# Head queries and keys taken straight from PSUM, a new order of the first phase, and a mix loaded by feature tiles

## The chip, the cores and the metric

The kernel runs on one core of a Trainium2 chip. The metric is the device time of one execution in microseconds; where several executions were timed, the median is given. The engines are named as in the profile: PE is TensorE (matmuls), DVE VectorE, ACT ScalarE, POOL GpSimd, SP SyncE, which issues nearly all transfers.

## The reference, cut to what matters

One layer of a streaming encoder runs over 1056 tokens: 1024 of a prompt and 32 of a running stream, 1024 features each. The layer has an adaLN modulation, one input projection shared by three groups of heads, an output projection with a LayerNorm, then a SwiGLU feed-forward part with another.

```python
h = x * (1 + sc1) + sh1
mq, mk, mv, mo, mi, mf, fq, fk, fv, ff, gu, gv = jnp.split(h @ w_in, split_at, axis=-1)
logf = jax.nn.log_sigmoid(ff + b_fox_f)          # gates of the attention heads
hm, (C1, n1, m1) = _mlstm(...)                   # 4 heads, chunks, decaying matrix memory
# 8 attention heads ("fox") of width 64, causal, with a forget term on the scores:
logits = q @ k.T * 64 ** -0.5 + Ft[:, None] - Ft[None, :]     # Ft = cumsum(logf)
hf = softmax(where(causal, logits, -inf)) @ v
hg = _spatial_gate(gu, layer_norm(gv), ws, bs)   # gMLP
mix = concat([hm, hf, hg], -1) @ w_o
x = layer_norm(ALPHA * x + (1 + g1) * mix)
```

The keys and values of the attention heads, the gates and the mLSTM's last state are outputs too (`o_kT` holds the keys).

## The kernel before

**Precision.** Each large product is done as three matmuls in the type fp32r. An operand is split into a high part (a cast by ACT) and a low part (the remainder, by DVE), and `gemm` (L111) multiplies hi·hi, hi·lo and lo·hi per tile of 128 features (L117 to L119). A weight tile of 512 KB is loaded and split in `weights` (L94; L105 on ACT, L106 on DVE).

**Memory.** Outputs of matmuls go to PSUM banks out of four pools: `pg` with three banks for projections, `pt` with two, `pss` with two for attention scores, `po` with one. A bank comes free when the last engine has read it. Tiles in the on-chip memory come from pools too; a pool that is closed gives its space to the one opened next, so that the later pool's first write waits for the earlier pool's last use. A pool's `bufs` is the length of a tile's ring.

**Order.** The program order is not the order in which the engines work: a scheduler in the compiler moves the instructions and then fixes, for each engine, one order in which it goes through its instructions; waits are on semaphores. `high_priority` puts a part ahead. The order of units in the first phase is the string `ORDER` (L42), read left to right by `run` (L1245): `q` a head's query/key projection, `f` the attention of one head over the first 512 tokens, `k0` and `k1p` the mLSTM's keys, `s` the states of the mLSTM (`mlstm_states`, L499), `v` and `o` the mLSTM's value and output-gate projections, `m` one of its chunks, `a` one unit of the adaLN modulation (`ada`, L171). `f` and `m` have high priority.

**Stages**, in the profile's times. Up to 105 us: modulation, the modulated tokens `h1`, the mLSTM's first projection, the value units. From 105 to 163: the first heads' projections and `gates` (L386). `gates` takes logarithms of the gates, cumulates them on PE (L426 and L427), then runs a long chain of small DVE operations (L433 to L487), stores the sums for the heads (`dfs`), d0 (`dd0`) and M (`dM`), and transposes the result on PE (L492) into `col`, whose exponential is L495. From 163 to 379: the eight heads' attention (`fox`, L672, `fox_chunk`, L699), woven with the mLSTM and from 290 on with the gMLP units (`tm_unit`, L272, with the evictions `evac_gv`, L343, and `evac_gmlp`, L639). From 379: the output projection of the first 512 tokens (`wo`, L942) with its LayerNorm; heads 4 to 7 of the other tokens until 462 us; then the feed-forward part.

**A head's way, before.** `fm_unit` (L236) computes 128 rows (64 of queries, 64 of keys) for pieces of 256 or 272 tokens. For heads 0 and 1 (`QD` = 2) all four pieces are done at once, for the others the first two, and the second two after the gMLP. `evac_qk` (L359) empties each bank: ACT writes the high part (L366), DVE the low part (L367), POOL their sum (L368), and three transfers store high, low and the keys. `fox` then loads from these stores what the scores need: `k1` (the keys' high part twice), `qp` (the queries' high and low part), `k2` and `q2` (the rest, with four rows of cumulated gates from `dfs`) and `v`, nine transfers in all. `foxbufs` (L1317) gives the rings of these tiles: k1 2, qp and q2 1, k2 1, v 3. They lie in the pool `mx0`, which is opened right after the gates' pool is closed. Each row of scores is two matmuls (L717 and L718) into a `pss` bank; DVE adds the mask and takes the maximum, ACT the exponential (L726). The probabilities are transposed on PE (L753) and multiplied by `v`; ACT and DVE add two halves (L773, L774) and the result is stored to `dmix`.

**The mix.** The three groups write the concatenated mix to DRAM (`dmix`). For the output projection, `wo_res` (L937) loads x (8 transfers of 256 KB), then `wo_mix` (L926) loads the mix: for each half of 256 tokens and each of the 8 feature tiles one transfer of 128 KB into a ring of four tiles, from which ACT writes the high part (L934) and DVE the low (L935). Feature tiles 2, 3, 4, 5, 0 and 1 are asked for first, 6 and 7 (the gMLP's) after the second pieces of heads 2 and 3.

Of the kernel before, what the change touches and what calls it, by code (L numbers as in the profile page):

```python
# [7 lines left out]
F32 = mybir.dt.float32  # L8
F32R = mybir.dt.float32r
AF = mybir.ActivationFunctionType  # L10
ALU = mybir.AluOpType
# [4 lines left out]
P = 128  # L16
D = 1024
KT = 8
# [7 lines left out]
QD = 2  # L26
# [12 lines left out]
MLB = (1, 2, 3, 4, 5)  # L39
RESE = "pp"  # L40
TAFF = ("aaaaaaaa", "aaaaaaav")
ORDER = "q0 f0 q1 a f1 a q2 f2 k0 k1p s a q3 f3 a v q4 f4 a q5 f5 o a m0 q6 f6 a m1 q7 m2 f7 a m3"  # L42
ADAPOS = 4
GENG = (0, 1, 1, 0)
FP = (0, 0)
# [20 lines left out]
def f(ap):  # L66
    return ap.bitcast(F32)


class Kernel:  # L70
# [288 lines left out]
    def evac_qk(self, h):  # L359
        nc = self.nc  # L360

        def evac(o, n, ps):
            hi = self.t(self.sm, [P, 272], F32R, "qkh", 3)
            lo = self.t(self.sm, [P, 272], F32R, "qkl", 2)
            kr = self.t(self.sm, [P, 272], F32, "qkr", 3)
            nc.scalar.activation(hi[:, :n], ps, AF.Copy, scale=self.qsc)  # L366
            nc.vector.scalar_tensor_tensor(lo[:, :n], ps, self.qsc, f(hi[:, :n]), ALU.mult, ALU.subtract)  # L367
            nc.gpsimd.tensor_tensor(kr[:, :n], f(hi[:, :n]), f(lo[:, :n]), ALU.add)  # L368
            self.store(self.dqh[h, :, o:o + n], f(hi[:, :n]))
            self.store(self.dql[h, :, o:o + n], f(lo[:, :n]))  # L370
            self.store(self.d["o_kT"][h, :, o:o + n], kr[64:, :n])
            if o + n == T:
                nc.gpsimd.tensor_copy(self.qks[:, h, :], kr[:, n - NS:n])
        return evac

    def evac_mqk(self, i, scale):
        nc = self.nc

        def evac(o, n, ps):
            r = self.t(self.sm, [P, 272], F32, "qkr", 3)  # L380
            nc.scalar.activation(r[:, :n], ps, AF.Copy, scale=scale)
            self.store(self.dmqk[:, i, o:o + n], r[:, :n])
        return evac
# [288 lines left out]
    def fox(self, h, chunks):  # L672
        self.phase = "fox"
        mx = self.mx
        q0, q1 = chunks[0][0] * P, (chunks[-1][-1] + 1) * P
        nq, nk, nb = q1 - q0, q1, q1 // P
        t = lambda shape, dt, tag, bufs: self.t(mx, shape, dt, tag, bufs)
        b = self.foxbufs
        k1 = t([P, nk], F32R, "k1", b[0])
        qp = t([P, nq], F32R, "qp", b[1])  # L680
        k2 = t([68, nk], F32R, "k2", b[2])
        q2 = t([68, nq], F32R, "q2", b[1])
        v = t([P, nb, P], F32R, "v", b[3])
        qs = slice(q0, q1)
        self.load(f(qp[0:64]), self.dqh[h, 0:64, qs])
        self.load(f(qp[64:128]), self.dql[h, 0:64, qs])
        self.load(f(k1[0:64]), self.dqh[h, 64:128, :nk])
        self.load(f(k1[64:128]), self.dqh[h, 64:128, :nk])
        self.load(f(q2[0:64]), self.dqh[h, 0:64, qs])
        self.load(f(q2[64:68]), self.dfs[h, 2:6, qs])  # L690
        self.load(f(k2[0:64]), self.dql[h, 64:128, :nk])
        self.load(f(k2[64:68]), self.dfs[h, 0:4, :nk])
        self.load(f(v), self.dv[:, :nb, h * P:(h + 1) * P])
        for tiles in chunks:
            o = tiles[0] * P - q0
            n = len(tiles) * P
            yield from self.fox_chunk(h, tiles, nk, n, k1, k2, qp[:, o:o + n], q2[:, o:o + n], v)

    def fox_chunk(self, h, tiles, W, nq, k1, k2, qp, q2, v):  # L699
        nc, mx = self.nc, self.mx  # L700
        nb = tiles[-1] + 1
        t = lambda shape, dt, tag, bufs: self.t(mx, shape, dt, tag, bufs)
        b5 = self.foxbufs[4]
        probs = []
        for i in tiles:
            n = (i + 1) * P
# [33 lines left out]
        o = self.t(self.po, [P, 512], F32, "o")  # L740
# [4 lines left out]
        for unit in units:  # L745
            ps = self.t(self.pt, [P, 512], F32, "t")
            at, e = [], 0
            for b in unit:
                first = max(0, b - tiles[0])
                w = nq - first * P  # L750
                for y in range(first, len(tiles)):
                    c = e + (y - first) * P
# [15 lines left out]
            self.phase = "fox"  # L768
        if held is not None:
            nc.tensor.matmul(o[:, :nq], v[:, 0, :], held[:, :nq], start=False, stop=True)  # L770
        tmp = t([64, nq], F32, "fo", 1)
        r = t([64, nq], F32, "fr", 1)
        nc.scalar.copy(tmp[:, :nq], o[64:128, :nq])  # L773
        nc.vector.tensor_tensor(r[:, :nq], o[0:64, :nq], tmp[:, :nq], ALU.add)  # L774
        c = tiles[0] // 4
        o = tiles[0] * P - GO[c]
        self.store(self.dmix[c][64 * (h % 2):64 * (h % 2) + 64, 2 + h // 2, o:o + nq], r[:, :nq])
# [148 lines left out]
    def wo_mix(self, c, ks):  # L926
        self.phase = f"wo{c}"
        nc = self.nc
        for a, b in MM[c]:
            for k in ks:  # L930
                r = self.t(self.p2, [P, 272], F32, "tmp", 4)[:, :b - a]
                self.load(r, self.dmix[c][:, k, a:b])
                h = self.hh[c][a][:, k, :b - a]
                nc.scalar.copy(h, r)  # L934
                nc.vector.tensor_tensor(self.hl[c][a][:, k, :b - a], r, f(h), ALU.subtract)  # L935
# [309 lines left out]
    def run(self):  # L1245
        nc, tc, d = self.nc, self.tc, self.d
        dr = self.pool("dr", space=DRAM)
        t = lambda shape, tag: self.t(dr, shape, F32, tag)
# [35 lines left out]
        w2, w3 = d["w_in"], d["w_in_f"]  # L1284
# [18 lines left out]
        def more(n):  # L1303
            for u in rest[:n]:
                self.ada(u, self.pl, "late", 2, self.pt, "t")
            del rest[:n]
# [7 lines left out]
        more(T1[3])  # L1314
        s2 = ExitStack()
        self.mx = self.pool("mx0", ctx=s2)
        self.foxbufs = (2, 1, 1, 2, 3)  # L1317

        def emit(x):
            eng = nc.gpsimd if x[-1] == "p" else nc.vector  # L1320
            x = x.rstrip("p")
            i = int(x[1:] or 0)
            if x[0] == "f":
                return self.fox(i, ((0, 1, 2, 3),))
            if x[0] == "m":
                return self.mlstm(i)
            if x[0] == "q":
                self.fm_unit(w3[2 + i], self.evac_qk(i), (0, 1) if i < QD else (0,), eng)
            elif x[0] == "k":
                self.fm_unit(w3[i], self.evac_mqk(2 + i, 0.125), eng=eng)  # L1330
            elif x[0] == "s":
                self.mlstm_states()
            elif x[0] == "a":
                more(1)
            else:
                self.tm_unit(w2["-vo".index(x)], 256, self.evac_raw((None, self.dmv, self.dmo)["-vo".index(x)]), eng=eng)
            return ()
# [12 lines left out]
        self.pz = self.pool("pz")  # L1350
        self.p2 = self.pada = self.pool("p2")
        self.hh, self.hl, self.z = {}, {}, {}
        self.wo_res(0, self.pz)
        self.operand(0, self.ph)
        self.wo_mix(0, self.KORDER[:6])
        def tail_ada():
            for u in rest:
                self.ada(u, self.wp, "raw", RAW, self.pg, "g")

        for i in range(4):  # L1360
            if i == ADAPOS:
# [102 lines left out]
        n = nj * 256  # L1464
        t = self.t(self.pz, [P, 4, n], F32R, "z0", 1)
        w = self.last_weights(((t[:, 0], t[:, 1]), (t[:, 2], t[:, 3])), (2, 3))
        act2 = dict(act)
        for half, (a, b) in enumerate(LN[1][::-1]):
# [6 lines left out]
            else:  # L1475
                h, l = (self.t(pb, [P, KT * 272], F32R, f"{x}{a}", 1) for x in ("ah", "al"))
# [111 lines left out]
```

## Time and profile before

| What | Value |
|---|---|
| Median of 3 runs | 1398.54 us (1397.95 to 1400.02) |
| Profiled execution, its own time | 1397.36 us |
| Its span in the trace | 1395.6 us |
| Mean granted clock of PE | 0.988 |
| From the first head projection to the output projection | 105.64 to 379.17 us |
| First matmul of the feed-forward part | 462.9 us |
| DMA engines, mean over the span | 167 GB/s |

Each line of the page's list of groups gives a source line, an engine, an operation with its tiles and its count, then the busy time, the mean of one in nanoseconds, and the idle time just before such instructions. A line of waits has the engine and the tile, after the arrow what released it, then the sum in microseconds, how often, and the longest. A line of a timeline begins with the start (us from the span's start) and the duration; a count at its end joins equal neighbours, and a bracket gives the idle time ahead and its releaser. A matmul's record overlaps with the next one's, so that durations of 0.28 us stand at starts 0.12 us apart: the spacing is what a matmul costs.

### The profile page before, as it was taken

Reading aid. Unit: us, or ns where it says so; the run is one execution under the profiler, and the core shown is the slowest. Engines: PE = TensorE matmul, PEld = TensorE weight load, DVE = VectorE, ACT = ScalarE, POOL = GpSimd, SP = SyncE. Lnnn points to the kernel's source line nnn. Section 1 sums busy time; section 2 is a strip of 40 time slices with the busy share of each in tenths; the row PEclk is TensorE's granted clock in tenths of the full one; section 3 lists DMA queues with packets and bytes.
Section 4 is the critical chain, followed back from the end, with each engine's and each line's share of the span. In section 5 each row is a group of like instructions: output and inputs, shape, how many; then the busy total and the mean of one; then the engine's idle time right before and its main releaser. Section 6 shows DMA issues by size and latency. Waiting matters only on the chain.

```text
span 1395.6 us, 25879 instructions
## 1 busy us (share of the span) xinstructions
PE 1346.8 (97%) x9651; PEld 1238.7 (89%) x9651; DVE 1034.0 (74%) x2198; ACT 641.6 (46%) x1257; POOL 258.7 (19%) x292
## 2 busy tenths in 40 slices
PE   7999999999979799999999999999999999999996
PEld 4899988899979778888887889899999999999996
DVE  5548646678779657777776766678997988888777
ACT  3313234445445444545544445344673544545355
POOL 0103200052146500000000000264620000000341
PEclk9999999999999899999999999999999999999998
DMA  9764577585755656444443342555597767563321
GB/s 360 255 219 134 171 234 210 176 253 168 225 174 158 186 174 178 128 131 138 137 131 85 100 119 83 198 153 139 157 237 202 204 174 199 149 174 112 101 91 65
DMA packets 134709, 233.09 MB, mean 167 GB/s; under 512 B 22436, under 2 KB 77356, under 8 KB 134584
## 3 DMA queue, kind: packets, MB, share of 16 engines
q1 hardware_dynamic: 129272, 221.34, 51.3%
q0 software_dynamic: 5168, 9.96, 4.6%
q8 instruction: 76, 1.25, 0.4%
q14 instruction: 49, 0.40, 0.1%
q10 hardware_dynamic: 144, 0.14, 0.0%
HBM read 197.50 MB, written 53.81 MB: 180 GB/s over the span
## 4 chain that ended last, share of the span: by engine, by line
PE 68%; DVE 4%; DMA 3%; issue 1%; ACT 1%; SPq 0%; POOL 0%; DVEq 0%; ACTq 0%
PE up_g L117 5%; PE up_g L118 5%; PE up_g L119 5%; PE dn_g L119 4%; PE dn_g L117 4%; PE dn_g L118 4%; PE sup_u L119 3%; PE sup_u L117 3%; PE sup_u L118 3%; PE wo_g L117 2%; PE wo_g L118 2%; PE wo_g L119 2%; PE sup_g L118 2%; PE sup_g L119 2%; PE sup_g L117 2%; PE fox_t L753 2%
## 5 line engine op out<-in xcount | busy, mean ns | idle before, releaser
L117 PE MATMUL up_g<-mlstm_ah,up_whi 128*128 128x512 f32 (+1 forms) x384 | 142.4, 371 | 4.3 <-ACT lna_tmp L996 3.4
L118 PE MATMUL up_g<-mlstm_al,up_whi 128*128 128x512 f32 (+1 forms) x384 | 142.8, 372 | 0.6 <-DVE mlstm_al L1001 0.6
L119 PE MATMUL up_g<-mlstm_ah,up_wlo 128*128 128x512 f32 (+1 forms) x384 | 142.2, 371 | 0.0
L284 PE MATMUL tm_g<-tm_whi,start_h1l 128*128 128x256 f32 (+1 forms) x384 | 110.0, 287 | 0.0
L282 PE MATMUL tm_g<-tm_whi,start_h1h 128*128 128x256 f32 (+1 forms) x384 | 109.6, 287 | 0.0
L283 PE MATMUL tm_g<-tm_wlo,start_h1h 128*128 128x256 f32 (+1 forms) x384 | 109.5, 286 | 0.0
L117 PE MATMUL fm_g<-start_h1h,fm_whi 128*128 128x256 f32 (+2 forms) x344 | 101.9, 301 | 4.7 <-DVE fm_qkl L367 2.0
L118 PE MATMUL fm_g<-start_h1l,fm_whi 128*128 128x256 f32 (+2 forms) x344 | 101.6, 295 | 0.2 <-DVE start_h1l L223 0.2
L119 PE MATMUL fm_g<-start_h1h,fm_wlo 128*128 128x256 f32 (+2 forms) x344 | 100.8, 294 | 0.0
L1120 ACT CAST sup_whi<-sup_raw 128x1024 fp32r<-128x1024 f32 x54 | 56.0, 1048 | 90.3 <-PE dn_u L118 46.7
L117 PEld LDWEIGHTS up_g<-mlstm_ah,up_whi 128*128 128x128 f32 x384 | 74.2, 193 | 16.6 <-ACT mlstm_ah L1000 3.5
L118 PEld LDWEIGHTS up_g<-mlstm_al,up_whi 128*128 128x128 f32 x384 | 74.3, 193 | 12.6 <-DVE up_actl L1054 0.8
L119 PEld LDWEIGHTS up_g<-mlstm_ah,up_wlo 128*128 128x128 f32 x384 | 74.4, 194 | 10.7
L105 ACT CAST up_whi<-up_raw 128x1024 fp32r<-128x1024 f32 x50 | 52.4, 1049 | 62.0 <-PE dn_g L118 22.5
L726 ACT ACTIVATE fox_p<-fox_s,fox_fmx 128x384 f32<-128x384 f32 (+2 forms) x96 | 55.1, 579 | 50.6 <-DVE fox_fmx L724 43.9
L1121 DVE TENSOR_TENSOR sup_wlo<-sup_raw,sup_whi 128x1024 fp32r<-128x1024 f32 x54 | 68.1, 1265 | 10.5 <-ACT sup_whi L1120 10.5
L117 PEld LDWEIGHTS fm_g<-start_h1h,fm_whi 128*128 128x128 f32 x344 | 65.4, 192 | 10.3 <-issue 2.9
L282 PEld LDWEIGHTS tm_g<-tm_whi,start_h1h 128*128 128x128 f32 x384 | 72.3, 189 | 1.9 <-issue 1.2
L106 DVE TENSOR_TENSOR up_wlo<-up_raw,up_whi 128x1024 fp32r<-128x1024 f32 x50 | 67.1, 1341 | 9.2 <-ACT up_whi L105 8.5
L284 PEld LDWEIGHTS tm_g<-tm_whi,start_h1l 128*128 128x128 f32 x384 | 72.3, 188 | 1.5 <-issue 1.2
L117 PE MATMUL dn_g<-up_acth,dn_whi 128*128 128x512 f32 (+2 forms) x200 | 73.5, 368 | 0.0
L118 PE MATMUL dn_g<-up_actl,dn_whi 128*128 128x512 f32 (+2 forms) x200 | 73.3, 368 | 0.0
(591 smaller groups left out, 4592.9 us busy)
## 6 DMA issues: line engine op xcount, KB each, us to landing
up_raw<-w_gu SPq DMA_DIRECT2D x50, 512.0 KB
dn_raw<-w_dn SPq DMA_DIRECT2D x28, 512.0 KB
ada_late<-w_ada SPq DMA_DIRECT2D x24, 512.0 KB
wo_raw<-w_o SPq DMA_DIRECT2D x24, 512.0 KB
sup_raw<-w_gu SPq DMA_DIRECT2D x20, 512.0 KB
start_dp<-w_gu SPq DMA_DIRECT2D x19, 512.0 KB
start_dp<-w_gu POOLq DMA_DIRECT2D x19, 512.0 KB, 7.9
sup_raw<-start_dp SPq DMA_DIRECT2D x18, 512.0 KB
```

What stands on the lines that cost most here:

```text
L105: nc.scalar.copy(hi[:, :w], raw[:, :w])
L106: (eng or nc.vector).tensor_tensor(lo[:, :w], raw[:, :w], f(hi[:, :w]), ALU.subtract)
L117: nc.tensor.matmul(ps, hi, xh(k), start=start and k == 0, stop=False)
L118: nc.tensor.matmul(ps, hi, xl(k), start=False, stop=False)
L119: nc.tensor.matmul(ps, lo, xh(k), start=False, stop=stop and k == n - 1)
L282: nc.tensor.matmul(ps[:, :ncol], xh, hi, start=k == 0, stop=False)
L283: nc.tensor.matmul(ps[:, :ncol], xh, lo, start=False, stop=False)
L284: nc.tensor.matmul(ps[:, :ncol], xl, hi, start=False, stop=k == 7)
L726: nc.scalar.activation(pr[:, lo:hi], banks[x][:, :hi - lo], AF.Exp, bias=mxs[:, 0:1], accum_out=sums[:, x:x + 1])
L753: nc.tensor.transpose(ps[:, c:c + P], probs[y][:, b * P:(b + 1) * P], self.ident)
L1120: nc.scalar.copy(h, x)
L1121: tt(l, x, f(h), ALU.subtract)
```

## The change

Four edits, all in the first phase:

1. `head_unit` takes the place of `fm_unit` for a head's first 512 tokens. It allots the head's tiles (k1, k2, qp, q2, v) in `mx0`, loads the gates' rows and v, runs one gemm of width 512 into one bank, and writes the tiles from that bank: ACT four copies (queries' high part, keys' high part twice, queries for q2), DVE two remainders. Two more ACT copies serve the store of the keys. Only the keys' high and low part are stored for later. `fox` uses the tiles and loads nothing. The rings become two for k1, k2, qp and q2; those of `qkh` and `qkr` go from three to two. Heads 0 and 1 keep their second pieces in the same unit.
2. `ORDER` is new: the mLSTM's key units, states and value unit come after head 1, its chunks after heads 2 to 5.
3. At the end of a head's attention the copy and the sum share one tile.
4. For the first 512 tokens `wo_mix` loads a whole feature tile (128 x 512, 256 KB) to the place of its low part, ACT copies it to the high part, DVE subtracts in place. `wo_res` stands after the first six of these.

```diff
-ORDER = "q0 f0 q1 a f1 a q2 f2 k0 k1p s a q3 f3 a v q4 f4 a q5 f5 o a m0 q6 f6 a m1 q7 m2 f7 a m3"
+ORDER = "q0 f0 q1 a f1 k0 k1p s a v q2 f2 a o a m0 q3 f3 a m1 q4 f4 a m2 q5 f5 a m3 q6 f6 a q7 f7"
...
-            hi = self.t(self.sm, [P, 272], F32R, "qkh", 3)
+            hi = self.t(self.sm, [P, 272], F32R, "qkh", 2)
...
+    def head_tiles(self, h, nq, nk):
+        b = self.foxbufs
+        t = lambda shape, tag, bufs: self.t(self.mx, shape, F32R, tag, bufs)
+        return (t([P, nk], "k1", b[0]), t([68, nk], "k2", b[2]), t([P, nq], "qp", b[1]), t([68, nq], "q2", b[1]),
+                t([P, nk // P, P], "v", b[3]))
+
+    def head_unit(self, h):
...
+        w = self.weights(self.d["w_in_f"][2 + h], KT, P)
+        self.phase = "head"
+        k1, k2, qp, q2, v = self.heads[h] = self.head_tiles(h, 512, 512)
+        self.load(f(q2[64:68]), self.dfs[h, 2:6, :512])
+        self.load(f(k2[64:68]), self.dfs[h, 0:4, :512])
+        self.load(f(v), self.dv[:, :4, h * P:(h + 1) * P])
+        ps = self.t(self.pg, [P, 512], F32, "g")
+        self.gemm(ps, w, slice(0, P), *self.h1parts(0, 512))
+        lo, hi = slice(0, 64), slice(64, 128)
+        nc.scalar.activation(qp[lo], ps[lo], AF.Copy, scale=0.125)
+        nc.vector.scalar_tensor_tensor(qp[hi], ps[lo], 0.125, f(qp[lo]), ALU.mult, ALU.subtract)
+        nc.scalar.copy(k1[hi], ps[hi])
+        nc.vector.tensor_tensor(k2[lo], ps[hi], f(k1[hi]), ALU.subtract)
+        nc.scalar.copy(k1[lo], ps[hi])
+        nc.scalar.activation(q2[lo], ps[lo], AF.Copy, scale=0.125)
+        for o in (0, 256):
+            kr = self.t(self.sm, [P, 272], F32, "qkr", 2)
+            nc.scalar.copy(kr[hi, :256], ps[hi, o:o + 256])
+            self.store(self.d["o_kT"][h, :, o:o + 256], kr[hi, :256])
+        self.store(self.dqh[h, hi, :512], f(k1[hi]))
+        self.store(self.dql[h, hi, :512], f(k2[lo]))
+        if h < QD:
+            evac = self.evac_qk(h)
+            self.phase = "fm"
+            for o, n in self.ranges((1,)):
+                ps = self.t(self.pg, [P, 512], F32, "g")
+                self.gemm(ps[:, :n], w, slice(0, P), *self.h1parts(o, n))
+                evac(o, n, ps[:, :n])
...
-        tmp = t([64, nq], F32, "fo", 1)
-        r = t([64, nq], F32, "fr", 1)
-        nc.scalar.copy(tmp[:, :nq], o[64:128, :nq])
-        nc.vector.tensor_tensor(r[:, :nq], o[0:64, :nq], tmp[:, :nq], ALU.add)
+        r = t([64, nq], F32, "fo", 1)
+        nc.scalar.copy(r[:, :nq], o[64:128, :nq])
+        nc.vector.tensor_tensor(r[:, :nq], o[0:64, :nq], r[:, :nq], ALU.add)
...
+        if c == 0:
+            for k in ks:
+                h, l = self.hh[0][0][:, k], self.hl[0][0][:, k]
+                self.load(f(l), self.dmix[0][:, k])
+                nc.scalar.copy(h, f(l))
+                nc.vector.tensor_tensor(l, f(l), f(h), ALU.subtract)
+            return
...
-        self.foxbufs = (2, 1, 1, 2, 3)
+        self.foxbufs = (2, 2, 2, 2, 3)
+        self.heads = {}
...
-                self.fm_unit(w3[2 + i], self.evac_qk(i), (0, 1) if i < QD else (0,), eng)
+                self.head_unit(i)
...
-        self.wo_res(0, self.pz)
         self.operand(0, self.ph)
         self.wo_mix(0, self.KORDER[:6])
+        self.wo_res(0, self.pz)
```

More of the change, by code (lines that the diff above doesn't have):

```diff
@@ L362, in evac @@
         def evac(o, n, ps):
-            hi = self.t(self.sm, [P, 272], F32R, "qkh", 3)
+            hi = self.t(self.sm, [P, 272], F32R, "qkh", 2)
             lo = self.t(self.sm, [P, 272], F32R, "qkl", 2)
-            kr = self.t(self.sm, [P, 272], F32, "qkr", 3)
+            kr = self.t(self.sm, [P, 272], F32, "qkr", 2)
             nc.scalar.activation(hi[:, :n], ps, AF.Copy, scale=self.qsc)
@@ L374, in evac_qk @@
         return evac
+    def head_tiles(self, h, nq, nk):
[4 more added lines that the diff above has]
+    def head_unit(self, h):
+        nc = self.nc
+        w = self.weights(self.d["w_in_f"][2 + h], KT, P)
[14 more added lines that the diff above has]
+        for o in (0, 256):
+            kr = self.t(self.sm, [P, 272], F32, "qkr", 2)
+            nc.scalar.copy(kr[hi, :256], ps[hi, o:o + 256])
[9 more added lines that the diff above has]
+                evac(o, n, ps[:, :n])
     def evac_mqk(self, i, scale):
@@ L379, in evac @@
         def evac(o, n, ps):
-            r = self.t(self.sm, [P, 272], F32, "qkr", 3)
+            r = self.t(self.sm, [P, 272], F32, "qkr", 2)
             nc.scalar.activation(r[:, :n], ps, AF.Copy, scale=scale)
@@ L676, in fox @@
         nq, nk, nb = q1 - q0, q1, q1 // P
[L677 to L693, printed above, removed]
+        if h in self.heads:
+            k1, k2, qp, q2, v = self.heads.pop(h)
+        else:
+            k1, k2, qp, q2, v = self.head_tiles(h, nq, nk)
+            qs = slice(q0, q1)
+            self.load(f(qp[0:64]), self.dqh[h, 0:64, qs])
+            self.load(f(qp[64:128]), self.dql[h, 0:64, qs])
+            self.load(f(k1[0:64]), self.dqh[h, 64:128, :nk])
+            self.load(f(k1[64:128]), self.dqh[h, 64:128, :nk])
+            self.load(f(q2[0:64]), self.dqh[h, 0:64, qs])
+            self.load(f(q2[64:68]), self.dfs[h, 2:6, qs])
+            self.load(f(k2[0:64]), self.dql[h, 64:128, :nk])
+            self.load(f(k2[64:68]), self.dfs[h, 0:4, :nk])
+            self.load(f(v), self.dv[:, :nb, h * P:(h + 1) * P])
         for tiles in chunks:
```

## The prediction

> **What bounds the kernel now.** I read the page first (busy shares, the span in 40 slices), then the table of stretches, then what TensorE's idle time waited for.
>
> ```profile
> span 1395.6 us, 25879 instructions
> PE 1346.8 (97%) x9651; PEld 1238.7 (89%) x9651; DVE 1034.0 (74%) x2198; ACT 641.6 (46%) x1257; POOL 258.7 (19%) x292
> PE   7999999999979799999999999999999999999996
> PEclk9999999999999899999999999999999999999998
> ```
>
> TensorE works 97% of the span, at nearly the full clock. A change can gain only by taking matmuls away, or by removing the few idle stretches; it can lose much by making new ones. The diff touches the stretch from about 105 to 402 us; in the changed kernel's instruction order TensorE's work from the first FFN matmul on is the same as before. So I cut that stretch (us, then PE, PEld, DVE, ACT, POOL busy, granted clock, DMA share, GB/s):
>
> ```profile
> 105.60:122.00 16.40, 16.40 (x140) 16.40 (x139) 11.98 (x31) 5.38 (x10) 3.57 (x6) 1.00 0.60 166
> 122.00:157.80 35.80, 33.83 (x268) 33.63 (x267) 34.19 (x81) 10.77 (x24) 15.43 (x21) 0.95 0.41 126
> 160.20:379.20 219.00, 212.59 (x1763) 196.78 (x1761) 142.85 (x416) 94.30 (x233) 39.85 (x48) 1.00 0.70 209
> 379.20:402.00 22.80, 15.32 (x106) 14.46 (x106) 13.03 (x22) 9.66 (x20) 5.19 (x7) 0.85 0.65 205
> ```
>
> Two things are to be seen. The first phase is dense: from 160.2 to 379.2 TensorE idles 219.0 − 212.6 = 6.4 us. And in 122 to 157.8 VectorE is busy 34.2 of 35.8 us with the gates' chain, while TensorE runs on: other matmuls cover that chain. The waits with a name:
>
> ```profile
> PE wo_g L117 <- ACT mlstm_ah L934: 5.5, 1, 5.5
> PE fm_g L117 <- DVE fm_qkl L367: 2.0, 1, 2.0
> PE fox_s L717 <- DMA fox_qp<-start_dql: 1.7, 1, 1.7
> PE fox_s L717 <- DMA fox_k<-start_dqh: 1.0, 1, 1.0
> ```
>
> The change can reach all four: 5.5 us for the mix at the output projection, 2.0 for a PSUM bank, 2.7 for fox operands that come back from DRAM.
>
> **The change part by part.** *Step 1: fewer matmuls.* One 512-wide group replaces two 256-wide ones, 24 matmuls for 48, in 8 heads. Spacing is from first and last of a row of starts (31 of width 256, 42 of 272, 16 of 512):
>
> ```profile
> 379.50 0.28 PE L119 MATMUL wo_g<-mlstm_ah,wo_wlo 128*128 128x256 f32 x1
> ...
> 383.08 0.28 PE L119 MATMUL wo_g<-mlstm_ah,wo_wlo 128*128 128x256 f32 x1
> 369.77 0.29 PE L117 MATMUL fm_g<-start_h1h,fm_whi 128*128 128x272 f32 x1
> ...
> 374.93 0.29 PE L119 MATMUL fm_g<-start_h1h,fm_wlo 128*128 128x272 f32 x1
> 630.19 0.39 PE L118 MATMUL dn_g<-up_actl,dn_whi 128*128 128x512 f32 x1
> ...
> 633.69 0.39 PE L118 MATMUL up_g<-mlstm_al,up_whi 128*128 128x512 f32 x1
> ```
>
> That is 3.58/30 = 0.119, 5.16/41 = 0.126 and 3.50/15 = 0.233 us. Gain: 8 × 24 × (2 × 0.119 − 0.233) = 1.0 us; the last digits of the spacings move that by some 0.4, and I take **−0.6**. That 192 matmuls go is hardly time, since the columns streamed are the same.
>
> *Step 2: the gates' chain loses its cover.* The head tiles are now the first tiles written in the pool opened after the gates, and this pool takes the gates' memory. In the changed instruction order ScalarE's first copy of head 0 therefore waits for VectorE's last gates instruction (today's L487), and VectorE's own head copies stand behind the whole chain. Three PSUM banks are all there are: head 0's and head 1's first halves hold two of them, so TensorE gets through q0's and q1's gemms, the first 32 gates matmuls and one more 272-wide gemm, then meets the transposes of L492, which need L487. Before, q1's rest and k stood in between. The rows:
>
> ```profile
> 119.46 0.38 PE L426 MATMUL gates_t<-start_tri,gates_gs 128*96 128x128 f32 x2
> ...
> 122.87 0.37 PE L117 MATMUL fm_g<-start_h1h,fm_whi 128*128 128x256 f32 x1
> 122.02 0.15 DVE L433 TENSOR_TENSOR gates_fc<-gates_fc,gates_rb 8x1 f32<-8x1 f32 x1 [1.89 <-ACT gates_rb L428]
> 156.21 0.15 DVE L479 TENSOR_TENSOR gates_d<-gates_m0x,gates_me 4x9 f32<-4x9 f32 x1
> 156.39 1.35 DVE L487 TENSOR_TENSOR gates_rs<-gates_rb,gates_me 4x1152 f32<-4x1152 f32 x1
> L367 DVE SCALAR_TENSOR_TENSOR fm_qkl<-fm_g,start_qsc,fm_qkh 128x256 fp32r<-128x256 f32 (+1 forms) x6 | 2.9, 477 | 0.2
> L106 DVE TENSOR_TENSOR fm_wlo<-fm_raw,fm_whi 128x1024 fp32r<-128x1024 f32 x1 | 1.2, 1207 | 0.0
> ```
>
> Start of the gates matmuls in the new order: 105.6 + 24 × 0.233 (5.6) + 48 × 0.126 (6.0) + 14 × 0.233 (3.3) = 120.5. The chain starts 2.5 us later (122.02 − 119.5), at 123.0. Its length is VectorE's 34.2 busy less head copies 2.9 and weights 1.2: 30.1 us, so it ends at about 153.5 with its small gaps. TensorE has 3.4 us of gates matmuls (119.46 to 122.87), the other 10 of q1 (2.3) and 24 × 0.126 (3.0), and is out of work at about 129.4. It idles **24 us**. Bounds: 19, if one bank comes free after all (24 matmuls of 233 ns less 0.6 of handing over, 5 us of cover); 27, if the last 272-wide gemm also finds no bank (3.0 us less cover).
>
> *Step 3: ScalarE behind a DMA round trip.* After the chain ScalarE has in order: two head-query copies, then the exponential of d0c (before's L513), which waits for d0's store and reload, and only then the keys' copies on which the first fox score waits. Matmuls between the chain and that score are nine transposes and one adaLN unit; I take 2.4 us for both, 9 × 0.272.
>
> ```profile
> 156.68 0.26 SPq L91 DMA_DIRECT2D start_dd<-gates_d  x1
> 163.69 0.22 ACT L513 ACTIVATE fm_d0c<-fm_d0c 128x18 f32<-128x18 f32 x1 [3.21 <-DMA fm_d0c<-start_dd]
> 165.07 0.37 ACT L182 COPY ada_adas<-ada_t 128x256 f32<-128x256 f32 x1 [0.40 <-PE ada_t L179]
> L492 PE MATMUL gates_t<-start_ident,gates_rs x9: 270/272/273, 160.2 to 163.5; 128*128 128x128 f32 x9
> 358.67 0.59 ACT L773 COPY fox_fo<-fox_o 64x512 f32<-64x512 f32 x1 [0.33 <-PE fox_o L770]
> ```
>
> From d0 written (156.36) to d0c's exponential it took 7.3 us; d0 is written some 1.4 us before the chain's end, so ScalarE is held to chain end + 5.9. Then two exponentials of some 0.25, three 64x512 copies of 0.59 and adaLN's 0.37 bring the first score to chain end + 8.6. Less the 2.4 of work: **+6.3** (3, if the round trip is quicker with SyncE's queue empty; 10, if the next adaLN unit waits too: its 512 KB stand on SyncE's queue behind d0c's and head 0's loads, which wait for the chain as well). ScalarE here waits with head copies queued behind it, and PSUM banks with them. The Trainium skill, in "TensorE: Matmul & The Clock Gate", Part 1 (Architectural detail), says that TensorE alone pulls weight loads ahead and that ScalarE and VectorE serve their queues strictly in order; it speaks against this change. By that rule the copies could not pass the exponential. The 3.21 us before L513 agree; no row here shows a pass.
>
> *Step 4: the clock.* After the 5.5 us wait the granted clock fell:
>
> ```profile
> 391.40:394.70 3.30, 3.29 (x15) 3.29 (x16) 1.57 (x4) 1.21 (x4) 0.00 (x0) 0.50 0.32 84
> ```
>
> 3.3 us at half rate cost 1.7 us. The idle of steps 2 and 3 is one stretch or two and brings one such window, **+1.7** (0 to 3.4). Before's own 2.0 us wait (L367's bank) and the clock of 0.95 behind it (0.05 × 35.8 = 1.8) fall away: **−3.7**. The Trainium skill, same page, Part 1 (What's actually happening), gives half rate after an idle window of about 3.4 us and full rate after a busy one; by it the price is also about 1.7 for each idle stretch longer than that (an estimate from the page's figures). The row agrees.
>
> *Step 5: fox without reloads, 160 to 379.* Nine loads a head become three, and the operand waits (2.7 us in the rows above) go. What comes instead: k1, k2, qp and q2 rings of two are filled by evictions, so head h+2's eviction waits until fox h's scores are done, and a PSUM bank is held that long; five head units stand almost back to back. With two score banks, four scores in a row have waits of their own. TensorE's 6.4 us of idle is all that can be won; what can be lost is below (rival 2). I take **0**, range −6.4 to +12.
>
> *Step 6: the mix by feature tiles.*
>
> ```profile
> 362.84 3.67 SPq L87 DMA_DIRECT2D mlstm_z<-xT  x8
> 386.96 4.82 SPq L87 DMA_DIRECT2D wo_tmp<-start_dmix  x4
> 390.09 1.61 ACT L934 CAST mlstm_ah<-wo_tmp 128x256 fp32r<-128x256 f32 x4 [4.91 <-DMA wo_tmp<-start_dmix]
> ```
>
> Before, the last loads are issued at 387, since each needs one of four ring tiles, and land around 390; three output groups of 18 matmuls run, then TensorE waits 5.5. Now each load goes to its own place, whole width, needs no ring, and passes the eight x loads on SyncE's queue; only tiles 6 and 7 come after the last stores. Sixteen copies of 256 become eight of 512. The x loads, now later on the queue, are first needed when an output group is evicted, 24 × 0.119 = 2.9 us into the stage; six mix loads ahead of them (4.82/4 = 1.2 us each to issue at worst, 7 us) put them at 370 instead of 363, still ahead of 379. The wait goes (−5.5) with its slow window (−1.7); the last two tiles, one store-and-load round trip behind, may bring 0 to 2 back; I take 1.2. **−6** (−9.2, if the rest of the 7.5 us idle goes too, to −3).
>
> *Sum:* −0.6 + 24 + 6.3 + 1.7 − 3.7 + 0 − 6 = **+21.7**. The profiled execution took 1397.36 (span 1395.6), which gives 1419.1; the runs' median is 1398.54, 1.2 above it, so about **1420**.
>
> **The rivals.** *1: faster, about 1395.* The matmuls that no longer cover the chain are still done later, so if the later stretch runs without a gap they lose nothing. Everything that is idle or slow here: 2.0 + 1.8, 6.4, 7.5 (22.8 − 15.3) with 1.7 for the clock, 0.6; and in 160 to 379 the 1763 records at 0.119 are 209.8 of 212.6 busy, another 2.8. Together 22.8. Against it stand steps 2 and 3 with their slow window, 1.7: the change gains where the two cost less than 21.1. With two banks let through under the chain (24 − 2 × 4.5 = 15) and 3 for step 3, the sum is 15 + 3 + 1.7 − 22.8 = −3.1: 1394.3, 1395 as a median. For it: the waits for operands and for the mix are truly removed. Against: all must come back at once, though step 5 adds bank holds.
>
> *2: heavier, about 1432.* Heads 5 to 7 hold the three PSUM banks until fox's scores go by, so the gMLP units wait for a bank, and VectorE gets dense:
>
> ```profile
> 295.50:379.20 83.70, 82.66 (x689) 79.17 (x688) 69.44 (x213) 38.62 (x96) 27.45 (x31) 1.00 0.64 194
> 293.42 0.42 DVE L347 BATCH_NORM_STATS2 tm_bst<-tm_g 128x6 f32<-128x256 f32 x1
> ...
> 295.58 0.55 DVE L352 TENSOR_SCALAR tm_traw<-tm_g,tm_bmv,tm_brs 128x256 f32<-128x256 f32 x1
> ```
>
> VectorE is already busy 83% there, and two fox heads more move into that part. A gMLP eviction holds its bank 2.7 us (293.42 to 296.13); about four units each exposed for 3 us cost 12: 1420 + 12. For it: in the changed order two gMLP gemms wait for head 5's and 6's evictions, and three for gMLP evictions. Against: fox's transposes and scores of other heads can lie beside these waits.
>
> *3: nearly all comes back, 1400 to 1404.* Steps 2 and 3 at 19 and 3, step 5 at −6.4, step 6 at −9.2: 19 + 3 + 1.7 − 3.7 − 6.4 − 9.2 − 0.6 = +3.8, 1402.4 as a median. It is the low tail of the forecast; it needs every uncertain term on one side.
>
> **How the numbers follow.** Forecast (1408 to 1427) 0.71; rival 2 0.15; rival 3 0.07; rival 1 0.07. Two kernels are told apart here from about 0.2%, 2.8 us: within it 0.05 (most of rival 3), faster 0.07, slower 0.88. Range 1401 to 1437: it leaves out rival 1, a part of rival 3 and a tail of rival 2, some 0.18 together.
>
> **What would show it.** After: TensorE idle from about 129 to 153 behind VectorE's last gates instruction, then 6 us behind ScalarE at the first fox score (steps 2, 3); half clock once behind it (4); no fox wait for DMA, but waits for evictions between 300 and 390 (5); no 5.5 us wait in the first output group (6). I am wrong if TensorE has matmuls under the chain after all, or if the first score starts right behind the transposes.

## The result and the profile after

The changed kernel takes 1419.76 us (1418.86 to 1420.46, 4 runs) where the kernel before takes 1399.28 (1397.95 to 1400.02, 4 runs): the ratio is 1.0145, 95% interval [1.0131, 1.0158], or some 20 us more. The forecast was 1420. The profiled execution took 1418.86 us. Its page, the lines that answer to those of before:

```profile
span 1416.6 us, 25406 instructions
PE 1345.4 (95%) x9459; PEld 1227.1 (87%) x9459; DVE 1028.2 (73%) x2190; ACT 657.5 (46%) x1281; POOL 241.7 (17%) x276
PE   7996599989999989999999999999999999999996
PEclk9998699999999999999999999999999999999998
```

TensorE's busy time is almost the same (1345.4 for 1346.8), and the span is 21.0 longer: the loss is idle time and slow clock. A slice is 35 us, and the fourth and fifth are the ones that changed. What TensorE waited for, in a table of the stretch from 100 to 430 us:

```profile
PE gates_t L530 <- DVE gates_rs L525: 23.5, 1, 23.5
PE wo_g L117 <- ACT tm_gms L703: 2.3, 1, 2.3
PE fox_s L752 <- ACT fox_p L761: 2.2, 3, 1.4
PE ada_t L185 <- ACT ada_adas L182: 2.0, 2, 1.8
PE ada_t L179 <- DMA ada_late<-w_ada: 1.4, 1, 1.4
```

The first line is the gates' transposes (L530 is before's L492) behind the last instruction of VectorE's gates chain (L525 is L487). No line names a reload of fox's operands, and the 5.5 us wait for the mix is gone. The place itself, from three timelines of after (VectorE, ScalarE, TensorE):

```profile
151.28 1.35 DVE L525 TENSOR_TENSOR gates_rs<-gates_rb,gates_me 4x1152 f32<-4x1152 f32 x1
152.67 1.07 ACT L394 ACTIVATE head_qp<-head_g 64x512 fp32r<-64x512 f32 x2 [14.11 <-DVE gates_rs L525]
157.30 0.22 ACT L551 ACTIVATE fm_d0c<-fm_d0c 128x18 f32<-128x18 f32 x1 [3.56 <-DMA fm_d0c<-start_dd]
152.78 2.15 PE L530 MATMUL gates_t<-start_ident,gates_rs 128*128 128x128 f32 x9 [23.50 <-DVE gates_rs L525]
159.97 0.79 PE L752 MATMUL fox_s<-head_k,head_qp 128*128 128x128 f32 x2 [0.53 <-ACT head_k L398]
162.77 1.08 PE L179 MATMUL ada_t<-ada_late,start_c 128*32 128x256 f32 x8 [1.39 <-DMA ada_late<-w_ada]
```

At 152.6 VectorE ends the chain; in the same tenth of a microsecond ScalarE writes the first head tile, after 14 us of waiting for that chain, and TensorE starts the transposes. The stretches of after (the columns as before), and under them the output projection's stretch of before:

```profile
129.00:152.80 23.80, 0.30 (x4) 0.11 (x2) 20.73 (x52) 1.30 (x5) 4.83 (x12) 0.61 0.04 7
152.80:165.00 12.20, 8.40 (x44) 5.07 (x45) 6.04 (x19) 6.66 (x17) 0.01 (x1) 0.50 0.58 168
165.00:170.00 5.00, 5.00 (x30) 4.61 (x31) 1.29 (x4) 1.23 (x3) 1.69 (x3) 0.68 0.47 141
165.00:200.00 35.00, 34.50 (x271) 32.37 (x270) 18.11 (x47) 14.63 (x36) 3.53 (x6) 0.95 0.61 186
300.00:345.00 45.00, 37.79 (x280) 32.40 (x280) 39.65 (x125) 22.40 (x60) 13.90 (x15) 0.96 0.57 166
400.00:412.60 12.60, 9.71 (x74) 9.08 (x72) 8.38 (x14) 6.00 (x10) 2.48 (x3) 1.00 1.02 360
412.60:488.20 75.60, 74.77 (x589) 73.81 (x589) 61.37 (x91) 39.21 (x69) 49.91 (x48) 0.98 0.62 188
```

```profile
379.20:462.90 83.70, 75.64 (x589) 74.08 (x588) 65.33 (x99) 42.32 (x79) 48.49 (x47) 0.96 0.58 175
```

The first row is the hole. Behind it TensorE's clock is 0.50 for 12 us more. The last row beside before's: the same 589 records, 8.1 us shorter. So 34.1 us are lost from the first head projection to the output projection (412.6 − 105.0 for 379.17 − 105.64), 8.1 are gained there, and 4.3 more after 488.

### The profile page after: what moved, and what is told of

Its sections match the earlier page's. It is cut to its first block, busy times and chain, and to the rows that moved or that the text cites. A ratio compares the mean times of both kernels' runs of the same rounds, so it can differ in the third digit from the quotient of the medians.

```text
span 1416.6 us, 25406 instructions
## 1 busy us (share of the span) xinstructions
PE 1345.4 (95%) x9459; PEld 1227.1 (87%) x9459; DVE 1028.2 (73%) x2190; ACT 657.5 (46%) x1281; POOL 241.7 (17%) x276
## 4 chain that ended last, share of the span: by engine, by line
PE 66%; DVE 4%; DMA 3%; ACT 2%; issue 1%; POOL 0%; SPq 0%; ACTq 0%; DVEq 0%
PE up_g L117 5%; PE up_g L118 5%; PE up_g L119 5%; PE dn_g L117 4%; PE dn_g L119 4%; PE dn_g L118 4%; PE sup_u L119 3%; PE sup_u L117 3%; PE sup_u L118 3%; PE wo_g L117 2%; PE wo_g L118 2%; PE wo_g L119 2%; PE sup_g L118 2%; PE sup_g L119 2%; PE sup_g L117 2%; PE fox_t L788 2%
## 5 line engine op out<-in xcount | busy, mean ns | idle before, releaser
L117 PE MATMUL up_g<-fox_ah,up_whi 128*128 128x512 f32 (+1 forms) x384 | 141.1, 368 | 4.1 <-ACT fox_ah L1041 3.4
L118 PE MATMUL up_g<-fox_al,up_whi 128*128 128x512 f32 (+1 forms) x384 | 141.3, 368 | 0.6 <-DVE fox_al L1042 0.6
L119 PE MATMUL up_g<-fox_ah,up_wlo 128*128 128x512 f32 (+1 forms) x384 | 140.5, 366 | 0.0
L117 PEld LDWEIGHTS up_g<-fox_ah,up_whi 128*128 128x128 f32 x384 | 72.8, 190 | 16.8 <-ACT fox_ah L1041 3.6
L118 PEld LDWEIGHTS up_g<-fox_al,up_whi 128*128 128x128 f32 x384 | 72.8, 190 | 12.0 <-DVE fox_al L1042 1.2
L119 PEld LDWEIGHTS up_g<-fox_ah,up_wlo 128*128 128x128 f32 x384 | 73.0, 190 | 10.6
L106 DVE TENSOR_TENSOR up_wlo<-up_raw,up_whi 128x1024 fp32r<-128x1024 f32 x50 | 66.7, 1333 | 14.7 <-ACT up_whi L105 14.0
L1016 DVE SCALAR_TENSOR_TENSOR wo_z<-dn_g,start_mod,wo_z 128x512 f32<-128x512 f32 (+4 forms) x120 | 60.3, 521 | 22.0 <-PE dn_g L119 21.3
L283 PEld LDWEIGHTS tm_g<-tm_wlo,start_h1h 128*128 128x128 f32 x384 | 72.8, 190 | 1.2 <-issue 0.4
L119 PE MATMUL dn_g<-up_acth,dn_wlo 128*128 128x512 f32 (+2 forms) x200 | 73.3, 366 | 0.0
L105 ACT CAST dn_whi<-dn_raw 128x1024 fp32r<-128x1024 f32 (+1 forms) x44 | 42.7, 971 | 50.1 <-PE up_g L118 11.3
```

Of the source, the lines that this page charges most:

```text
L105: nc.scalar.copy(hi[:, :w], raw[:, :w])
L106: (eng or nc.vector).tensor_tensor(lo[:, :w], raw[:, :w], f(hi[:, :w]), ALU.subtract)
L117: nc.tensor.matmul(ps, hi, xh(k), start=start and k == 0, stop=False)
L118: nc.tensor.matmul(ps, hi, xl(k), start=False, stop=False)
L119: nc.tensor.matmul(ps, lo, xh(k), start=False, stop=stop and k == n - 1)
L283: nc.tensor.matmul(ps[:, :ncol], xh, lo, start=False, stop=False)
```

## The experiments

My theory: the loss is the memory wait (steps 2 to 4), some 30 us; the rest of the change is about even. The rival: the order of the units and the banks that head units hold cost it. The comparisons ran on several chips, on which before's median was 1393.8 to 1399.3; so the ratio counts. The table gives it with three lengths from each profiled run, in us: from the first head projection to the first output matmul, from there to the first feed-forward matmul, and from the first head projection to the start of fox's last product in this phase.

| Kernel | Ratio to before | To output | Output | To fox's end |
|---|---|---|---|---|
| before | 1 | 273.5 | 83.7 | 252.5 |
| after | 1.0145 [1.0131, 1.0158] | 307.6 | 75.6 | 288.7 |
| 1 own pool | 1.0025 [1.0008, 1.0042] | 281.6 | 84.9 | 274.0 |
| 2 heads 0, 1 as before | 1.0016 [1.0002, 1.0029] | 278.2 | 82.2 | 266.0 |
| 3 before, new mix | 0.9942 [0.9923, 0.9961] | 273.7 | 75.7 | 251.8 |
| 4 states late | 1.0166 [1.0149, 1.0183] | 308.1 | 75.5 | 289.1 |
| 5 own pool, old order | 1.0077 [1.0053, 1.0101] | 299.3 | 73.8 | 271.3 |
| 6 before, new order | 1.0078 [1.0048, 1.0107] | 289.3 | 79.7 | 276.0 |
| 7 as 2, old order | 1.0100 [1.0075, 1.0125] | 297.2 | 73.6 | 267.5 |
| 8 d0's exponential first | 1.0154 [1.0125, 1.0182] | 307.9 | 75.4 | 288.9 |
| 9 own pool, x first | 1.0045 [1.0029, 1.0061] | 288.6 | 78.4 | 273.9 |
| 10 as 9, heads 4 to 7 as before | 1.0092 [1.0073, 1.0111] | 293.9 | 77.2 | 279.2 |
| 11 before, new mix, x first | 0.9959 [0.9941, 0.9976] | 275.5 | 74.8 | 253.6 |
| 12 as 3, shared tile, rings of two | 0.9962 [0.9947, 0.9978] | 278.2 | 74.1 | 256.2 |

### 1 and 2: the memory wait taken away

```diff
         more(T1[2])
+        s2 = ExitStack()
+        self.hp = self.pool("hp", ctx=s2)
         self.gates()
...
-        s2 = ExitStack()
         self.mx = self.pool("mx0", ctx=s2)
```

with k1, k2, qp and q2 of the first 512 tokens taken from `hp` and v from `mx0`.

> The kernel after, but the tiles k1, k2, qp and q2 of the heads lie in a pool of their own that is opened ahead of the gates, so that they do not take the gates' memory; nothing else is changed. Theory (the loss is the memory wait): TensorE's 23.5 us in front of the gates' transposes and most of the 9 us behind them go, no wait of TensorE over 3 us is left between 105 and 165, and the time falls by 26 to 31 us to 1389 to 1394, below the kernel before. Rival (the order of the units or the banks held by head units cost the time, the memory only shows it): the chain stays uncovered or the wait moves to fox, 1408 to 1420.

Experiment 2 leaves the pools and does two heads the old way, `self.fm_unit(w3[2 + i], self.evac_qk(i), (0, 1), eng)` for i < 2.

> The kernel after with heads 0 and 1 done as before (fm_unit, stores, reloads); heads 2 to 7, the order and the mix stay as in after. Theory: the gates' chain is covered again, and the first fox scores no longer stand behind d0c's exponential: 1390 to 1395. Rival (what costs is the holding of PSUM banks by the six later head units and the dense VectorE): 1405 to 1418.

In both the hole is gone: no wait of TensorE for the chain is left, and the way to the output is 26.0 and 29.4 us shorter than in after. In the own-pool kernel the first fox scores even stand at 117 us, ahead of the chain:

```profile
117.06 0.39 PE L753 MATMUL fox_s<-head_k,head_qp 128*128 128x128 f32 x2
```

So the memory wait was the cause of the hole. But the time fell by 1.2% of 1397, 17 us, and not by 26 to 31: the output stretch became 9.3 us longer. In both experiments the time lies between the range of the theory and that of the rival. The longest waits at the output projection, in the own-pool kernel and in experiment 2 (there 5.6 us stand ahead of the first output matmul, the rest behind it):

```profile
PE wo_g L117 <- DVE fm_qkl L367: 4.4, 1, 4.4
```

```profile
PE wo_g L117 <- ACT fox_ah L967: 8.0, 2, 5.6
```

Own pool, two timelines (ScalarE, then SyncE):

```profile
399.90 0.62 ACT L968 CAST fox_ah<-fox_al 128x512 fp32r<-128x512 f32 x1 [8.20 <-DMA fox_al<-start_dmix]
381.30 0.45 SPq L91 DMA_DIRECT2D start_dmix<-fox_fo  x1
382.88 2.77 SPq L87 DMA_DIRECT2D fox_al<-start_dmix  x6
385.69 5.70 SPq L87 DMA_DIRECT2D wo_z<-xT  x8
396.06 1.02 SPq L87 DMA_DIRECT2D fox_al<-start_dmix  x2
```

The last head's result is stored at 381.3, the mix loads follow, and the first output matmul is due at 387.1. Fox's end moved up by only 14.7 us (288.7 to 274.0) when the way to the output got 26.0 shorter. In after TensorE arrives 18.8 us behind fox's last product (412.6 − 393.8), in the own-pool kernel 7.6: the hole had hidden that fox ends late.

### 3 and 11: the mix alone

> The kernel before with the mix's part of the change alone: feature tiles of 512 for the first tokens, six of them ahead of the x loads. Theory: the 5.5 us wait in the first output group and the half clock behind it go, some 6 us: 1391 to 1394. Rival (the wait only moves to the last two feature tiles, which stand behind the last stores): 1397 to 1400.

> The kernel before with feature tiles of 512 for the mix, but with the x loads left ahead of it: half of the third experiment (ratio 0.9942). Theory (the ring of four tiles made the wait, the place on the queue did not): 0.993 to 0.996. Rival (the place ahead of the x loads is what gains): 0.997 to 1.000.

The edit of 3 is part 4 of the change on the kernel before; 11 leaves `wo_res` ahead of `wo_mix`. The output stretch is 75.7 and 74.8 us for 83.7. The ratio 0.9942 is 8.1 us of 1397, where 6 were forecast; without the new place on the queue it is 0.9959, with an interval that overlaps. So the loads through the ring of four tiles were most of it (the ring and the half-width tiles went together and were not tried apart); whether the place adds 2 us stays open. Experiment 3 beats both kernels.

### 4 and 8: ScalarE behind d0c's reload

> The kernel after with the mLSTM's states asked for later (s behind the o unit, ahead of m0), so that the exponential of d0c no longer stands on ScalarE ahead of head 0's key copies. The 23.5 us stay. Theory (step 3, ScalarE behind a DMA round trip): the first fox score comes 2 to 4 us sooner after the chain, 1416 to 1418. Rival (the round trip is not what the first score waits for; the copies themselves and the slow clock are): within 1 us of 1419.8.

> The kernel after, but d0's exponential is taken on its 4x9 tile ahead of the store, so that nothing on ScalarE waits for d0c's reload; the values are the same. Moving the states in the program order had left ScalarE's order as it was. The 23.5 us stay. Theory (step 3): the first fox score, 7.2 us after the chain's end in after, comes 2 to 4 us sooner; the time falls by 1 to 4 us, ratio 1.011 to 1.014. Rival (VectorE's remainders and the adaLN unit set the first score, not the reload): it comes at most 1 us sooner, ratio as after, 1.0145.

Experiment 4 has `s` behind `o` in the order; the build left ScalarE's order as it was, so it tells nothing on step 3 and only shows that after's ratio returns. Experiment 8:

```diff
+        nc.scalar.activation(d0, d0, AF.Exp)
         self.store(self.dd0, d0)
...
-        nc.scalar.activation(self.d0c, self.d0c, AF.Exp)
```

Its timeline of ScalarE around the chain's end, and two lines of TensorE's waits:

```profile
153.00 1.07 ACT L394 ACTIVATE head_qp<-head_g 64x512 fp32r<-64x512 f32 x2 [1.17 <-DVE gates_rs L526]
155.51 0.29 ACT L534 ACTIVATE start_col<-start_col 128x108 f32<-128x108 f32 x1 [1.44 <-DVE start_col L532]
156.22 0.58 ACT L396 CAST head_k<-head_g 64x512 fp32r<-64x512 f32 x1 [0.42 <-DVE head_qp L395]
...
PE gates_t L531 <- DVE gates_rs L526: 23.5, 1, 23.5
PE ada_t L179 <- DMA ada_late<-w_ada: 2.7, 1, 2.7
```

The wait for the reload is gone, and the first score comes at 159.0, 6.0 us behind the chain's end instead of 7.3: 1.3 us. ScalarE now waits for VectorE, which has the transposes' copies and the remainders first. And the wait for adaLN's weights is 2.7 instead of 1.4: what was won is waited for there. The ratio, 1.0154 with an interval from 1.0125, is that of after and decides nothing between the two; the trace does. With 1.3 us the rival (at most 1) is nearer than the theory (2 to 4): the reload was the smaller part of the term.

### 5, 6 and 7: order against head units

The own pool removed the hole and still left 0.8% between it and experiment 3. There are two candidates: the order, and the head units.

> The kernel after with the head tiles in their own pool (as in the first experiment) and with the ORDER of before; head units, rings and the new mix stay. Measured so far: the own pool alone gives a ratio to before of 1.0025, the mix alone 0.9942, after 1.0145. In the own-pool kernel the last fox product comes 274 us after the first head projection, before 253 us, so that the mix is late again at the output projection. Theory (the new order is the second cost: it asks for heads 2 to 7 later, and fox's end is then late): with the old order the ratio is 0.990 to 0.995, 1382 to 1389 where before takes 1396. Rival (the head units themselves cost it, by PSUM banks held and by copies on ScalarE and VectorE): 1.000 to 1.005.

> The kernel before with the new ORDER alone; head projections, rings and the mix as before. Theory (the order delays fox): the last fox product of this stage comes 15 us or more later than before's 253 us after the first head projection, the wait for the mix at the output projection grows, ratio 1.004 to 1.012. Rival (head units are the cost, the order is harmless): 0.998 to 1.002.

> The kernel after with heads 0 and 1 done as before and with the old ORDER; heads 2 to 7 are head units without reloads, the mix is new. Theory (order): ratio 0.990 to 0.996. Rival (head units): 1.000 to 1.004, as with the new order (1.0016).

The edits are the one line `ORDER`. Experiment 6 came as forecast: the new order alone puts fox's end at 276.0 for 252.5 and costs 0.8%. Experiments 5 and 7 refute the rest of that theory: with the old order the head units cost more, not less, and both ratios lie above the ranges of theory and rival. One line of each kernel's waits (5, 7, 6):

```profile
PE gates_t L531 <- DVE gates_rs L526: 12.4, 1, 12.4
```

```profile
PE gates_t L530 <- DVE gates_rs L525: 12.0, 1, 12.0
```

```profile
PE wo_g L117 <- ACT fox_ah L934: 12.9, 1, 12.9
```

With the old order and head units half of the hole is back, in 5 though the memory is no longer shared. In TensorE's instruction order of 5 and 7 there stand, behind the rest of head 1, head 2's gemm and two pieces of k0 between the gates matmuls and the transposes; in before's there are two pieces of head 2 and six of the key units. Old-style units are emptied to DRAM and cover the chain; a head unit is emptied into rings of two tiles that fox must free first, and holds its PSUM bank until then. In 7 head 2's gemm is done at 138 us, and ScalarE's first copy of its bank is released by fox's scores 29 us later:

```profile
167.00 0.59 ACT L394 ACTIVATE head_qp<-head_g 64x512 fp32r<-64x512 f32 x1 [1.07 <-PE fox_s L752]
```

The new order puts k0 and k1p under the chain, which covers it, and pays at the other end: fox is late, and the mix with it. That the rings are the reason for the open 12 us was read from the orders and this line and not tried by itself: on ScalarE d0c's exponential, which waits for the chain too, also stands ahead of that copy.

### 9 and 10: the late mix

> The own-pool kernel (first experiment, ratio 1.0025) with the eight x loads put back ahead of the mix loads, as in before. In the own-pool trace the last fox product stands 7.6 us ahead of the output projection, the x loads take SyncE from 385.7 to 391.4 behind the six mix loads, the stores of heads 2 and 3 wait behind them, and VectorE's L367 at 397 waits for such a store; TensorE waits 4.4 us for that PSUM bank, and the stage from the first output matmul to the feed-forward part takes 85.0 us instead of 75.5 in after. Theory (the change's new place of the x loads takes the way of the stores once fox is late): that stage takes 78 to 81 us and the ratio falls to 0.997 to 1.000. Rival (fox's late end itself is the cost, whatever stands on the queue): the wait moves to the mix, the ratio stays 1.001 to 1.004.

> As the run before, but heads 4 to 7 as in the kernel before (stores and reloads), heads 0 to 3 as head units. Theory (step 5: PSUM banks and rings held by the late head units cost some 5 to 8 us between the first head projection and the output projection): that stretch, 281.6 us in the own-pool kernel, falls to 274 to 278. Rival (the reloads cost as much as the held banks, since fox's end is what counts): 279 us or more, or a wait of several us for the mix at the output projection as with the old head units in the new order (12.9 us).

In 9 the output stretch fell to 78.4 as expected, but a wait came in front of it, and the sum of both stretches is 367.0 for 366.5: this speaks for the rival, fox's late end. In 10, reloads for heads 4 to 7 put fox's end back by 5 us more. The first line of waits, of 9 and of 10:

```profile
PE wo_g L117 <- ACT fox_ah L968: 7.0, 1, 7.0
```

```profile
PE wo_g L117 <- ACT fox_ah L968: 13.2, 1, 13.2
```

So heads 4 to 7 as head units bring something on balance, 5 us at fox's end. What their banks cost by themselves this run can't tell. In after's trace rival 2's wait is not there: between 300 and 412 us TensorE waits 0.2 us for the eviction of a gMLP projection, where rival 2 had 12, and then 2.3 for one of the gMLP's copies ahead of the first output matmul.

### 12: two parts kept

> The kernel before with two parts of the change, the mix by feature tiles and the shared tile at the end of a head's attention, and with the space of the latter given to rings of two for qp and q2, so that a head's queries are loaded while the head before still uses its own. Theory (the waits of fox for operands, 2.4 us in the third experiment, are on the path): they go, ratio 0.990 to 0.993. Rival (what is gained there is lost to the next wait): as the third experiment, 0.994.

The edit is parts 3 and 4 of the change on before, and `foxbufs` (2, 2, 1, 2, 3). The largest fox wait, in 12 and in 3:

```profile
PE fox_s L718 <- DMA fox_k<-start_dql: 2.9, 1, 2.9
```

```profile
PE fox_s L717 <- DMA fox_qp<-start_dql: 2.4, 2, 1.6
```

The wait for the queries went and one for the keys' low part came, whose ring is still one. Nothing is gained over 3; the theory falls.

## Why the prediction was right, point by point

- **Step 2, the memory wait: right.** Forecast 24 us, measured 23.5; the chain's end forecast at 153.5, measured 152.6, and experiment 1 shows the cause. What the sum did not say is that the price is not what the removal returns: 17 us, since fox's late end comes out from behind it.
- **Steps 3 and 4: 9.6 us for 8.0, and the second was too small.** Step 3 took the time up to the first score less 2.4 us of work at full clock. From the transposes' start (152.78) to that score (159.97) it is 7.2 us, and the 4.8 us that TensorE is busy in them are 2.4 us of work at half clock: 4.8 for the 6.3 forecast. The reload is 1.3 of it (experiment 8); the rest is copies on ScalarE and VectorE, and the slow clock. The next adaLN unit's wait, which step 3 had as its worst case, came with 1.4. Step 4 is what failed: behind the first score TensorE is busy another 3.6 us up to 165 and 3.2 up to 168.2 at half clock, and half of that is 3.4 us where one window, 1.7, was forecast. By idle time and clock alone, the same 9.6 us are 12.2 − 8.4 = 3.8 of idle time and 5.8 of clock (half of 8.4 and of 3.2, an estimate). TensorE works in short pieces behind the hole, and the clock came back only behind a stretch without a gap:

```profile
163.80:168.20 4.40, 4.40 (x23) 4.40 (x20) 0.50 (x2) 0.86 (x2) 1.70 (x3) 0.50 0.55 159
168.20:170.00 1.80, 1.80 (x16) 1.41 (x17) 0.79 (x3) 0.37 (x1) 0.00 (x0) 1.00 0.58 177
```

  The Trainium skill, "TensorE: Matmul & The Clock Gate", Part 1 (What's actually happening), asks for a sustained busy window of about 3.4 us before full rate; 8.4 busy in 12.2 were not enough here, which agrees.
- **Step 5, fox: forecast 0, measured +4.2 of idle time and 1.6 of clock.** TensorE's idle time between 165 and 412.6 is 0.5 us up to 200, 7.2 in 300 to 345 and 2.9 in 400 to 412.6 (none from 200 to 300 and from 345 to 400), 10.6 for the 6.4 of before; and from 311.6 to 315.0 the clock is halved once more. The 7.2 are not the waits for evictions that were forecast for 300 to 390: they are mostly waits of 1.0 to 1.4 us for fox's and the mLSTM's own steps. Of the 2.9, 2.3 are the wait for the gMLP's copy ahead of the first output matmul. Experiments 1, 3 and 6 show a larger part that the sum missed: the order delays fox's end by 23 us, and with a covered chain order and head units together cost 0.83%, 11.6 us (1 against 3). In after that lies behind the hole.
- **Step 6, the mix: forecast −6, measured −8.1**, alone (experiment 3) as in after.
- **Step 1, fewer matmuls: forecast −0.6, about −1.2.** From the first head projection to the output projection TensorE is busy 265.2 us before and 269.7 after. Less half of its busy time at half clock (1.7 and 7.4 us) that is 263.4 and 262.2, an estimate:

```profile
105.64:379.17 273.53, 265.15 (x2186) 249.14 (x2184) 190.19 (x528) 110.49 (x267) 58.85 (x75) 0.99 0.65 194
```

```profile
105.04:412.63 307.59, 269.67 (x1993) 242.77 (x1992) 189.59 (x528) 129.03 (x299) 42.18 (x58) 0.94 0.49 147
```

- **Not in the sum: −4.3 us** from the first feed-forward matmul on, where both kernels do the same matmuls in the same order. TensorE's idle time there is the same, 21.9 and 22.2 us; the clock differs. Before has it halved in 473.2 to 476.6, 480.1 to 486.9 and 753.1 to 760.0, after only in 499.3 to 502.7. Half of the busy time in these windows is 7.9 and 1.7 us, an upper estimate, so the clock is enough for the 4.3. The last of before's windows stands behind a stall at one of fox's scores, which after has too, but shorter (before's stall, its window and after's stall):

```profile
753.60 0.69 PE L717 MATMUL fox_s<-fox_k,fox_qp 128*128 128x384 f32 x1 [2.50 <-ACT fox_p L726]
753.12:759.95 6.83, 6.35 (x17) 5.28 (x18) 5.13 (x11) 3.67 (x11) 0.72 (x1) 0.50 0.52 166
```

```profile
776.78 0.45 PE L752 MATMUL fox_s<-fox_k,fox_qp 128*128 128x384 f32 x1 [1.78 <-ACT fox_p L761]
```

  The 14 kernels' traces agree at this score: the clock was halved behind stalls of 2.50, 2.38, 2.21, 1.99 and 1.80 us (before and experiments 3, 11, 2 and 6), and stayed full in the other nine, whose stalls were at most 1.78.

The sum of what was measured: 23.5 + 9.6 − 3.7 (before's own wait and slow clock there) + 4.2 + 1.6 − 1.2 − 8.1 − 4.3 − 0.6 (the stage begins that much sooner) = 21.0, and the spans differ by 21.0; a few tenths of that agreement hang on the estimates of the clock. The forecast's direction, its main term and that term's cause were right. That 21.7 came so close to 21.0 was luck: the sum had some 7.4 us too little (1.6 for steps 3 and 4, 5.8 for fox) and some 8 too much (0.5 for the hole, 0.6 for the matmuls, 2.1 for the mix, 4.3 and 0.6 of which it had nothing).

Rival 1 (all of the cover comes back) is refuted as a whole by experiment 1, ratio 1.0025: even without the hole the change does not gain, for what the order and the head units cost together. Rival 2 named a late stretch correctly, but not its mechanism: TensorE hardly waited for the gMLP's banks, and reloads for the late heads (experiment 10) made it worse.

## What to carry to other kernels

Before a tile moves to a newly opened pool, ask whose memory it takes and what stands behind that owner's last use: here a 30 us chain off the critical path came onto it through one shared address range. Units that are emptied to DRAM covered such a chain here; units emptied into short rings covered only half of it with the old order (their rings are the likely reason, not a tried one), and the order that covered it made the last consumer end late. Do not price a stall by its length: with a hole of 33 us gone, slow clock included, the time fell by 17.

## What the runs showed of the hardware

In the idle stretch of 23.5 us the granted clock fell to 0.50, 5 us in (0.61 over the stretch). It stayed there while TensorE was busy 69% of the 12 us behind the stretch, in short pieces, and was 1.00 again at 168.2, after 4.4 us of work without a gap. The half clock from the transposes on cost 5.8 us (an estimate: half of the busy time), 2.4 of them ahead of the first score, where TensorE also waited for ScalarE.

Stalls much shorter than that can cost the clock too. At one and the same score of the later work, 14 traces show stalls of up to 2.50 us: behind the five of 1.80 us and more the clock was halved for 3.4 to 6.8 us, behind the nine of at most 1.78 it was not. This is no fixed limit: at other places of these traces, stalls of 1.86 us (experiment 11, at 202 us) and of 2.14 us (after, at 528 us) left the clock at 1.00.
